# The order of tokens in the last two gate groups of each half of a streaming-encoder layer

## The chip, the cores and the metric

The kernel runs as one program on one core of a Trainium2 chip; the metric is the device time of one execution in microseconds (us). The core has a matmul engine (TensorE, PE in the rows, with its weight loads PEld), a vector engine (VectorE, DVE), an activation engine (ScalarE, ACT), a general engine (GpSimd, POOL) and SyncE (SP), whose queue issues every DMA of this kernel.

## The reference

One encoder layer over 2048 tokens of width 1024. A layer norm gives `h`. One input projection of 7592 columns feeds three branches: A, attention over the 256 keys with the highest score of a small indexer (top-k per query); B, differential attention with 4 heads; C, attention of 4 heads into 256 memory tokens. Each branch has a SiLU gate of 512 columns, an output projection to 1024 columns and a sigmoid gate of 1024 columns:

```
proj = h @ w_in[l]
...
y_a = (o_a * jax.nn.silu(a_gate)) @ w_proj_a[l]
...
g = jax.nn.sigmoid(m_gate.reshape(bsz, seq, N_BRANCH, D_MODEL))
merged = g[:, :, 0] * y_a + g[:, :, 1] * y_b + g[:, :, 2] * y_c
h = _layer_norm(DEEPNORM_ALPHA * h + merged @ w_out[l], ln_g[l], ln_b[l])
```

## The kernel before

All large matmuls are done in three parts of a high and a low half (`mm3`, lines 76 to 79: high by high, high by low, low by high), so one product is three matmuls.

The normalised input, transposed, lives in the tile `H4` (line 153; the rows call it `H`). It has room for 1024 tokens, one half of the sequence, in two parts of 512 tokens, `H4[:, 0]` and `H4[:, 1]`, each with high and low parts. The first half's tokens are computed first, stored to memory as `ht_d` (four pieces of 256 tokens and 2 MB), and the second half takes their place. At the end the second half is used up and the four pieces are read back by `reload` (line 210), two into each part of `H4`.

What the text calls gate groups are the 20 entries of `JOBS` (lines 390 to 392): 256 columns each of the C queries (`cq`, 2), the SiLU gates (`sg`, 6) and the merge gates (`tm`, 12). `gate_steps` (line 260) does one: it loads the 256 columns of weights (`load_win`, line 228: in the second half raw from memory, split into high and low by GpSimd and stored; in the first half read back in one piece of 2 MB as `w<-w_d`), and then for each part of 512 tokens of the half and each 128 columns it runs 24 matmuls of 512 columns into one of two PSUM tiles `dps`. `emit_gate` (line 313) empties it through a tile `do`, of which there are three, and SP stores that: for `tm` with one ScalarE pass, for `sg` with one more on VectorE, for `cq` with one `do` from ScalarE (line 318) and one from VectorE (line 321).

The order of the program text is: projections of half 0, top-k, projections of half 1, top-k for the blocks 8 to 15 (`topk_group`, on VectorE, ScalarE and GpSimd), then at line 793 all 20 gate groups of half 1, the four `reload`, and four gate groups of half 0. The next 12 are `fill` (line 798), steps put between the matmuls of branch B's attention by hand (`pump`, in a region in which the order of TensorE is that of the text). Branch B's tiles (`bp`, line 635) take the place of the top-k's, and its keys, values and queries (`kg`, `vg`, `bq`) are loaded there.

Then comes branch A's attention (`attn_a`, line 852, 16 blocks), what is left of `fill`, and at line 917 the last four gate groups of half 0. Between them stands the projection of the memory tokens: `gates` (line 394) calls one entry of its list `between` after each group and the rest of the list after the last group. The list is `mem_setup` (loads and transposes the memory tokens into `hm`, pool `mp`) and four times `dense_mem` (line 417: four loads of raw weights through two buffers `wr`, eight GpSimd instructions that split them into a tile `w`, 48 matmuls of 256 columns in all, two stores of `mk_d` or `mv_d`). All users of weights share two buffers `w` in turn.

Then the pools of this phase are given back and those of the next (`yp`, `yw`, `yq`, lines 921 to 923) take their place. The next phase loads the projection weights of branches B and C through tiles `yt` (eight buffers) and splits them on ScalarE and VectorE into the two parts of `H4`: `wb` into `H4[:, 0]`, `wc` into `H4[:, 1]` (lines 957 to 959). For each of 8 pairs of blocks it multiplies branch B's output by its gate (`gated`, line 937, with `yo` in one buffer), projects it (`branch`, into `yps`), then does branch C's attention and its projection.

Outside of the hand-ordered region a planner puts each engine's instructions in one fixed order: it simulates the program with its own durations and takes, at each step, the instruction that is ready with the highest priority. Priority is the order of the text, raised inside `tc.high_priority()`. So branch A's attention and the gate groups after it in the text are interleaved on TensorE, and so are branch A's attention and the phase after them. On the chip each engine runs its fixed order and waits where a datum or a buffer is late. A tile that takes the place of another waits for that tile's users alone.

Of the kernel before, what the change touches and what calls it, by code (L numbers as in the profile page):

```python
# [44 lines left out]
GB = (4, 12)  # L45
# [13 lines left out]
def tile_layer(ctx, tc, x, mem, ln_in_g, ln_in_b, w_in, w_mem_kv, diff_lambda, diff_norm_g,  # L59
# [7 lines left out]
    def split(H, L, src, eh, el):  # L67
        if eh is G:
            G.tensor_scalar(H, src, 1.0, 1.0, op0=ALU.mult, op1=ALU.mult)  # L69
        elif eh is A:  # L70
            A.copy(H, src)  # L71
        else:
            V.tensor_copy(H, src)
        el.tensor_tensor(L, src, H.bitcast(F32), op=ALU.subtract)  # L74

    def mm3(ps, lH, lL, rH, rL, start, stop):
        PE.matmul(ps, lH, rH, start=start, stop=False)  # L77
        PE.matmul(ps, lH, rL, start=False, stop=False)  # L78
        PE.matmul(ps, lL, rH, start=False, stop=stop)  # L79
# [3 lines left out]
    def dram(name, shape, dt=F32):  # L83
        return dr.tile(shape, dt, name=name)
# [59 lines left out]
    def w_view(w, r0, nk, c0, n):  # L144
        return bass.AP(tensor=w.tensor, offset=w.offset + r0 * w.shape[-1] + c0,
                       ap=[[w.shape[-1], 128], [128 * w.shape[-1], nk], [1, n]])

    def pool(name, bufs, space=None, side="left"):
        kw = {} if space is None else {"space": space}
        return tc.alloc_tile_pool(name=name, bufs=bufs, side=side, reuse_waits="tile", **kw)  # L150
# [77 lines left out]
    def load_win(cols, eh=G, el=G, rpool=None):  # L228
        w = dw.tile([128, 2, KT, 256], F32R, name="w")
        key = cols[0][0]  # L230
        if key in w_d:
            SP.dma_start(w.bitcast(F32), w_d[key])
            return w
        n = sum(c for _, c in cols)
        m = 2 if rpool is None else 4
        for i in range(0, KT, m):
            raw = (rpool or dw).tile([128, m, 256], F32, name="wr", bufs=2)
            o0 = 0
            for c0, cn in cols:
                SP.dma_start(raw[:, :, o0:o0 + cn], w_view(w_in, i * 128, m, c0, cn))  # L240
                o0 += cn
            split(w[:, 0, i:i + m, :n], w[:, 1, i:i + m, :n], raw[:, :, :n], eh, el)
        w_d[key] = dram(f"w_d{key}", [128, 2, KT, 256])
        SP.dma_start(w_d[key], w.bitcast(F32))
        return w
# [11 lines left out]
            with tc.high_priority():  # L257
                emit(kind, idx, p, ps, n)

    def gate_steps(kind, half, c0, idx):  # L260
        w = load_win([(c0, 256)])
        for q in range(2 * half, 2 * half + 2):
            for g in range(2):
                c = slice(g * 128, (g + 1) * 128)
                ps = dqs.tile([128, 512], F32, name="dps")
                for k in range(KT):
                    mm3(ps, w[:, 0, k, c], w[:, 1, k, c], H4[:, q % 2, 0, k], H4[:, q % 2, 1, k], k == 0, k == KT - 1)
                    if k == KT - 1:
                        with tc.high_priority():
                            emit_gate(kind, idx, g, q, ps)  # L270
                    yield 0.69
# [41 lines left out]
    def emit_gate(kind, idx, g, q, ps):  # L313
        if kind == "cq":
            for a in range(2):
                o = dw.tile([128, 512], F32R, name="do", bufs=3)
                if a == 0:
                    A.copy(o, ps)
                    H = o
                else:  # L320
                    V.tensor_tensor(o, ps, H.bitcast(F32), op=ALU.subtract)
                SP.dma_start(cq_d[q][:, 2 * idx + g, a], o.bitcast(F32))
            return
        r, j = idx
        o = dw.tile([128, 512], F32, name="do", bufs=3)
        A.activation(o, ps, AF.Tanh, scale=0.5)
        if kind == "sg":
            V.scalar_tensor_tensor(o, o, 1.0, ps, op0=ALU.add, op1=ALU.mult)  # L328
        SP.dma_start((sg_d if kind == "sg" else tm_d)[r][q][:, 2 * j + g], o)
# [60 lines left out]
    JOBS = [("cq", C_CQ + 256 * j, j) for j in range(2)]  # L390
# [3 lines left out]
    def gates(half, jobs, between=()):  # L394
        between = list(between)
        for i, (kind, c0, idx) in enumerate(jobs):
            yield from gate_steps(kind, half, c0, idx)
            if between:
                between.pop(0)()
        for f in between:  # L400
            f()

    def run(steps):
        for _ in steps:
            pass
# [11 lines left out]
    def dense_mem(j):  # L417
        w = dw.tile([128, 2, KT, 256], F32R, name="w")
        for i in range(2):
            for k in (4 * i, 4 * i + 2):  # L420
                raw = dw.tile([128, 2, 256], F32, name="wr", bufs=2)
                SP.dma_start(raw, w_view(w_mem_kv, k * 128, 2, 256 * j, 256))
                split(w[:, 0, k:k + 2], w[:, 1, k:k + 2], raw, G, G)
        ps = dqs.tile([128, 2, 256], F32, name="dps")
        for i in range(2):
            c = slice(i * 128, (i + 1) * 128)
            if j < 2:
                for k in range(KT):
                    mm3(ps[:, i], w[:, 0, k, c], w[:, 1, k, c], hm[0][:, 0, k], hm[0][:, 1, k], k == 0, k == KT - 1)
            else:  # L430
                for k in range(KT):
                    mm3(ps[:, i], hm[0][:, 0, k, c], hm[0][:, 1, k, c], w[:, 0, k], w[:, 1, k], k == 0, k == KT - 1)
        for i in range(2):
            o = dw.tile([128, 2, 256], F32R, name="do", bufs=3)
            if j < 2:
                split(o[:, 0], o[:, 1], ps[:, i], A, V)
                SP.dma_start(mk_d[:, 2 * j + i], o.bitcast(F32))
            else:
                h0 = 2 * (j - 2)
                ov = o.rearrange("p a (h d) -> p (a h d)", d=128).rearrange("p (h a d) -> p h a d", h=2, a=2)  # L440
                pv = ps[:, i].rearrange("p (h d) -> p h d", d=128)
                split(ov[:, :, 0], ov[:, :, 1], pv, A, V)
                SP.dma_start(mv_d[:, i, h0:h0 + 2].rearrange("p h a d -> p (h a d)"),
                             o.bitcast(F32).rearrange("p a c -> p (a c)"))
# [252 lines left out]
    class unit_b:  # L697
# [78 lines left out]
        def store(self):  # L776
# [13 lines left out]
            G.tensor_scalar(o, o, rs, None, op0=ALU.mult)  # L790
            SP.dma_start(ob_d[b][:, hd * 128:(hd + 1) * 128], o)

    run(gates(1, JOBS))
    for p in range(4):
        with tc.high_priority():
            reload(p)
    run(gates(0, JOBS[:GB[0]]))
    fill = gates(0, JOBS[GB[0]:GB[0] + GB[1]])
    owed = [0.0]

# [12 lines left out]
    with tc.manual_schedule(engines={PE.engine}):  # L813
# [5 lines left out]
        for i, u in enumerate(units):  # L819
# [8 lines left out]
            j = 0  # L828
# [85 lines left out]

    run(fill)
    mp = pool("mp", 1)
    run(gates(0, JOBS[GB[0] + GB[1]:], [mem_setup] + [(lambda j=j: dense_mem(j)) for j in range(4)]))
    mp.release()
    dqs.release()
    dw.release()  # L920
# [264 lines left out]
```

## Time and profile before

| | before |
|---|---|
| time, median of 3 runs | 2924.34 us (2923.38 to 2928.38) |
| the profiled execution | 2925.13 us, of which the span is 2923.3 us |
| TensorE busy | 2778.1 us (95%) |
| VectorE busy | 2053.1 us (70%) |
| ScalarE busy | 1401.7 us (48%) |
| GpSimd busy | 864.6 us (30%) |
| mean granted TensorE clock | 0.982 |
| moved by DMA | 476.35 MB, 163 GB/s over the span |

The time is that of the whole execution; the span is what the hardware profiler covers, from the first instruction to the last. Times in rows count from the start of the span. Busy time counts instructions of the engine itself, without waits. The granted clock is 1.00 at the upper of TensorE's two levels (2.4 GHz) and lower where part of a stretch ran at the other (1.2 GHz).

### The profile page before, as it was taken

The numbers are of one execution on the slowest core, as the hardware profiler recorded it, in microseconds if no ns is written. First come the engines' busy times: TensorE is split into PE (matmuls) and PEld (weight loads), VectorE is DVE, ScalarE is ACT, GpSimd is POOL, SyncE is SP. The second block draws the span as 40 slices with busy tenths as digits, with TensorE's granted clock in tenths as the row PEclk, the third lists the DMA queues.
The fourth block names the chain that finished last, engine by engine and source line by source line (L and its number), as shares of the span: only waits on it lengthen the run. The fifth ranks groups of instructions, "written<-read, shape, count | busy, mean of one in ns | idle before, by whom it ended". The sixth has DMA issues, their size and how long they took to land.

```text
span 2923.3 us, 49093 instructions
## 1 busy us (share of the span) xinstructions
PE 2778.1 (95%) x17488; PEld 2490.2 (85%) x17488; DVE 2053.1 (70%) x4885; ACT 1401.7 (48%) x2716; POOL 864.6 (30%) x1270
## 2 busy tenths in 40 slices
PE   6899999999999989999999998998999999988998
PEld 6799989987788877788888887887999899987887
DVE  7179978898657887677777773447777777775554
ACT  3256755774346870344444442446555655552010
POOL 7454333235433302022222323121222222211322
PEclk9999999999999999999999999999999999998999
DMA  9666555564554576434334335235333333358542
GB/s 359 233 210 237 202 179 172 169 231 171 201 173 167 190 268 203 148 114 142 109 120 131 119 99 160 97 118 170 104 104 99 118 113 111 117 170 268 198 155 73
DMA packets 332020, 476.35 MB, mean 163 GB/s; under 512 B 28928, under 2 KB 252544, under 8 KB 323584
## 3 DMA queue, kind: packets, MB, share of 16 engines
q1 hardware_dynamic: 331776, 473.23, 49.5%
q8 instruction: 138, 2.26, 0.3%
q14 instruction: 106, 0.87, 0.1%
HBM read 271.25 MB, written 201.88 MB: 162 GB/s over the span
## 4 chain that ended last, share of the span: by engine, by line
PE 68%; DMA 7%; DVE 6%; issue 3%; POOL 2%; ACT 2%; SPq 1%; POOLq 0%; DVEq 0%; ACTq 0%
PE dps L77 9%; PE dps L78 9%; PE dps L79 9%; PE ops L753 4%; PE aops L898 4%; PE apt L893 3%; PE lg L648 3%; PE lg L649 3%; PE yps L77 2%; PE yps L78 2%; PE yps L79 2%; PE pt L761 2%; PE fz L77 2%; PE fz L78 2%; PE fz L79 2%
## 5 line engine op out<-in xcount | busy, mean ns | idle before, releaser
L77 PE MATMUL dps<-H,w 128*128 128x512 f32 x1280 | 518.5, 405 | 20.0 <-DVE do L328 5.7
L78 PE MATMUL dps<-H,w 128*128 128x512 f32 x1280 | 505.6, 395 | 0.0
L79 PE MATMUL dps<-H,w 128*128 128x512 f32 x1280 | 504.2, 394 | 0.0
L77 PE MATMUL dps<-w,H 128*128 128x256 f32 (+1 forms) x1152 | 342.1, 298 | 15.4 <-ACT w L71 8.6
L79 PE MATMUL dps<-w,H 128*128 128x256 f32 (+1 forms) x1152 | 339.8, 296 | 2.3 <-DVE H L74 2.3
L78 PE MATMUL dps<-w,H 128*128 128x256 f32 (+1 forms) x1152 | 340.7, 296 | 0.8 <-POOL w L74 0.8
L556 ACT ACTIVATE ja<-sall,thr 128x1280 bf16<-128x1280 f32 (+4 forms) x224 | 301.9, 1348 | 74.7 <-DVE thr L552 69.1
L543 DVE TENSOR_SCALAR_CACHE_REDUCE jd<-sall,thr 128x1408 bf16<-128x1408 f32 (+6 forms) x231 | 330.8, 1432 | 6.3
L77 PEld LDWEIGHTS dps<-H,w 128*128 128x128 f32 x1280 | 243.8, 190 | 64.8 <-issue 9.7
L79 PEld LDWEIGHTS dps<-H,w 128*128 128x128 f32 x1280 | 243.1, 190 | 51.2
L78 PEld LDWEIGHTS dps<-H,w 128*128 128x128 f32 x1280 | 243.8, 190 | 38.2
L651 DVE CUSTOM_DVE_ANT_0 AP<-lg,bias 128x512 f32<-128x512 f32 (+3 forms) x304 | 181.8, 619 | 124.7 <-PE lg L649 61.5
L516 DVE SCALAR_TENSOR_TENSOR sall<-ir,iw,sall 128x512 f32<-128x512 f32 (+3 forms) x266 | 191.9, 768 | 70.6 <-ACT ir L512 68.1
L77 PEld LDWEIGHTS dps<-w,H 128*128 128x128 f32 x1152 | 223.5, 194 | 18.1 <-ACT w L71 9.3
L71 ACT CAST apr<-apt 128x512 fp32r<-128x512 f32 (+1 forms) x288 | 157.5, 562 | 160.7 <-PE apt L893 129.5
L79 PEld LDWEIGHTS dps<-w,H 128*128 128x128 f32 x1152 | 223.1, 194 | 3.5 <-DVE H L74 2.7
L78 PEld LDWEIGHTS dps<-w,H 128*128 128x128 f32 x1152 | 223.5, 194 | 3.0 <-POOL w L74 2.2
L74 DVE TENSOR_TENSOR apr<-apt,apr 128x512 fp32r<-128x512 f32 (+1 forms) x288 | 185.5, 656 | 57.1 <-ACT apr L71 55.4
L898 PE MATMUL aops<-apr,VA 128*128 128x256 f32 x1088 | 209.0, 299 | 14.9 <-ACT apr L71 6.5
L69 POOL TENSOR_SCALAR w<-wr 128x512 fp32r<-128x512 f32 x120 | 87.1, 734 | 424.7 <-PE dps L79 339.2
L885 ACT ACTIVATE AP<-AP,anm 128x1024 f32<-128x1024 f32 (+7 forms) x192 | 172.1, 900 | 67.7 <-DVE anm L882 64.1
L512 ACT ACTIVATE ir<-ips 128x512 f32<-128x512 f32 (+3 forms) x304 | 150.0, 550 | 105.4 <-PE ips L507 92.0
(250 smaller groups left out, 6835.9 us busy)
## 6 DMA issues: line engine op xcount, KB each, us to landing
w_d<-w SPq DMA_DIRECT2D x28, 2048.0 KB, 7.3
w<-w_d SPq DMA_DIRECT2D x28, 2048.0 KB, 8.8
wr<-in_w_in_dram SPq DMA_DIRECT2D x108, 256.0 KB, 3.3
tm_d<-do SPq DMA_DIRECT2D x96, 256.0 KB, 2.9
bq<-qb_d SPq DMA_DIRECT2D x128, 128.0 KB, 3.3
aq<-qa_d SPq DMA_DIRECT2D x128, 128.0 KB, 3.1
yt<-tm_d SPq DMA_DIRECT2D x64, 256.0 KB, 3.5
sg_d<-do SPq DMA_DIRECT2D x48, 256.0 KB, 2.6
```

What stands on the lines that cost most here:

```text
L71: A.copy(H, src)
L74: el.tensor_tensor(L, src, H.bitcast(F32), op=ALU.subtract)
L77: PE.matmul(ps, lH, rH, start=start, stop=False)
L78: PE.matmul(ps, lH, rL, start=False, stop=False)
L79: PE.matmul(ps, lL, rH, start=False, stop=stop)
L512: A.activation(r[:, :cn], ps[:, :cn], AF.Relu)
L516: V.scalar_tensor_tensor(s[:, c0:c0 + cn], r[:, :cn], iw[:, h:h + 1], s[:, c0:c0 + cn], op0=ALU.mult, op1=ALU.add)
L543: V.tensor_scalar(jd[:, :L], sc[b], t.bitcast(F32)[:, i:i + 1], None, op0=op, op1=ALU.add, accum_out=dst[:, i:i + 1])
L556: A.activation(ja[:, :L], sc[b], AF.Sign, bias=thr.bitcast(F32)[:, i:i + 1], scale=-1.0, accum_out=cnt[:, i:i + 1])
L651: V.tensor_tensor_reduce(P[:, c0:c0 + cn], ps[:, :cn], bias[:, c0:c0 + cn], scale=-0.125, scalar=-LOW, op0=ALU.add, op1=ALU.min, accum_out ...
L885: A.activation(p[:, c0:c1], p[:, c0:c1], AF.Exp, bias=nm[:, e:e + 1], scale=-1.0, accum_out=sm[:, hd, i:i + 1])
L898: PE.matmul(o_ps.rearrange("p a d -> p (a d)"), VA[:, k0 + i], pr[:, a, i].rearrange("p e q -> p (e q)"), start=(k0 + i == 0 and a == 0), ...
```

## The change

The last two gate groups of each half are taken out of `gates` and given to a new function. It loads the weights of both groups, then runs the first 512 tokens of the first group, the first 512 of the second, the second 512 of the first and the second 512 of the second. `gate_steps` takes the weights and the list of parts as arguments. Since `gates` now gets two groups at line 917 and still the list of five entries, it calls three `dense_mem` after its second group, so these stand in the text ahead of the last two gate groups.

```
-    def gate_steps(kind, half, c0, idx):
-        w = load_win([(c0, 256)])
-        for q in range(2 * half, 2 * half + 2):
+    def gate_steps(kind, half, c0, idx, w=None, qs=(0, 1)):
+        if w is None:
+            w = load_win([(c0, 256)])
+        for q in (2 * half + q for q in qs):
...
+    def gates_by_tokens(half, jobs):
+        ws = [load_win([(c0, 256)]) for _, c0, _ in jobs]
+        for q in range(2):
+            for (kind, c0, idx), w in zip(jobs, ws):
+                yield from gate_steps(kind, half, c0, idx, w, (q,))
...
-    run(gates(1, JOBS))
+    run(gates(1, JOBS[:-2]))
+    run(gates_by_tokens(1, JOBS[-2:]))
     for p in range(4):
         with tc.high_priority():
             reload(p)
...
-    run(gates(0, JOBS[GB[0] + GB[1]:], [mem_setup] + [(lambda j=j: dense_mem(j)) for j in range(4)]))
+    run(gates(0, JOBS[GB[0] + GB[1]:-2], [mem_setup] + [(lambda j=j: dense_mem(j)) for j in range(4)]))
+    run(gates_by_tokens(0, JOBS[-2:]))
     mp.release()
```

## Rows read from the trace of the kernel before

**Rows 1.** The page, part 1 and the chain's shares by engine (part 4).

```profile
PE 2778.1 (95%) x17488; PEld 2490.2 (85%) x17488; DVE 2053.1 (70%) x4885; ACT 1401.7 (48%) x2716; POOL 864.6 (30%) x1270
...
PE 68%; DMA 7%; DVE 6%; issue 3%; POOL 2%; ACT 2%; SPq 1%; POOLq 0%; DVEq 0%; ACTq 0%
```

**Rows 2.** First hand-over by stretch: length, PE, PEld, DVE, ACT, POOL, clock, DMA, GB/s.

```profile
1055.46:1066.30 10.84, 10.84 (x48) 8.64 (x47) 9.36 (x15) 8.93 (x10) 0.00 (x0) 1.00 0.92 281
1066.30:1070.90 4.60, 0.01 (x1) 0.01 (x1) 3.86 (x6) 3.87 (x4) 0.00 (x0) 0.82 1.08 362
1070.90:1084.50 13.60, 13.58 (x49) 11.01 (x50) 10.81 (x18) 9.23 (x12) 0.00 (x0) 0.81 1.11 370
1084.50:1100.28 15.78, 12.84 (x50) 10.13 (x49) 14.46 (x34) 6.83 (x8) 0.00 (x0) 0.89 0.50 198
```

**Rows 3.** The longest wait of TensorE, 990 to 1120 us: total, times, longest.

```profile
PE dps L77 <- DMA H<-ht_d: 4.6, 1, 4.6
```

**Rows 4.** SP's issues in order of time: start, us, what.

```profile
1044.59 0.32 SPq L232 DMA_DIRECT2D w<-w_d  x1
...
1055.46 3.49 SPq L211 DMA_DIRECT2D H<-ht_d  x2
...
1066.34 5.54 SPq L211 DMA_DIRECT2D H<-ht_d  x2
1071.94 6.30 SPq L232 DMA_DIRECT2D w<-w_d  x1
```

**Rows 5.** The chain that ended last, 1000 to 1300 us: start, us, what.

```profile
1056.10 14.69 DMA H<-ht_d
...
1080.45 10.43 DMA cq_d<-do
...
1177.38 5.17 DMA bq<-qb_d
1182.68 0.77 PE lg L649
```

**Rows 6.** ScalarE in order of time; in brackets idle time before, and releaser.

```profile
1079.12 0.59 ACT L318 CAST do<-dps 128x512 fp32r<-128x512 f32 x1 [2.73 <-PE dps L79]
...
1091.56 1.05 ACT L318 CAST do<-dps 128x512 fp32r<-128x512 f32 x2
```

**Rows 7.** VectorE, the end of the top-k.

```profile
1156.85 0.68 DVE L594 TENSOR_SCALAR pf<-ja 128x2048 bf16<-128x2048 bf16 x1
```

**Rows 8.** SP's issues at the start of branch B and after the gate groups.

```profile
1157.93 1.76 SPq L679 DMA_DIRECT2D kg<-kb_d  x2
...
1966.55 1.28 SPq L932 DMA_DIRECT2D yt<-in_w_proj_b_dram  x3
...
1978.20 0.67 SPq L1016 DMA_DIRECT2D yo<-ob_d  x1
```

**Rows 9.** TensorE in order of time, second hand-over.

```profile
1948.44 0.40 PE L79 MATMUL dps<-H,w 128*128 128x512 f32 x1
...
1966.23 0.28 PE L79 MATMUL dps<-w,hm 128*128 128x256 f32 x1
...
1998.04 0.60 PE L942 MATMUL cps<-idf,yo 128*128 128x128 f32 x4
...
2003.05 0.39 PE L78 MATMUL yps<-yoT,H 128*128 128x256 f32 x1 [0.88 <-POOL yoT L946]
```

**Rows 10.** Busy time by stretch, second hand-over (columns as in rows 2).

```profile
1948.67:1966.35 17.68, 17.68 (x144) 17.43 (x143) 6.75 (x17) 6.23 (x13) 7.49 (x8) 1.00 0.33 105
1966.35:2003.05 36.70, 28.07 (x162) 22.47 (x160) 30.70 (x71) 28.05 (x57) 2.55 (x2) 0.86 1.00 317
```

**Rows 11.** GpSimd, first and last split of one `dense_mem`.

```profile
1948.93 1.20 POOL L69 TENSOR_SCALAR w<-wr 128x512 fp32r<-128x512 f32 x2 [26.17 <-PE dps L79]
...
1957.82 1.29 POOL L74 TENSOR_TENSOR w<-wr,w 128x512 fp32r<-128x512 f32 x1
```

**Rows 12.** The page, part 6: a load of 256 KB, KB each, median us to landing.

```profile
yt<-tm_d SPq DMA_DIRECT2D x64, 256.0 KB, 3.5
```

## The prediction

> **What bounds the kernel now.** The page comes first: TensorE is busy for 95% of the span and holds 68% of the chain that ended last; no other engine is above 70% or 6% [rows 1]. So the time is TensorE's work plus the places where it stands still or runs at its lower clock, and the change adds or removes no matmul. Next come the two hand-overs that it touches, read by stretch.
>
> First hand-over: the last gate groups of half 1 end at 1066.30. TensorE then does nothing for 4.6 us, waiting for the read-back of `H` [rows 2, 3]. The first group of half 0 takes from 1070.90 to 1100.28, where a group takes 4 x 5.42 = 21.7 us (48 matmuls, half a group, in 10.84 us) [rows 2]. In all 1100.28 - 1066.30 - 21.7 = 12.3 us are lost: 4.6 idle, 2.9 idle in the last stretch (15.78 less 12.84), and 4.8 at the lower of the two clock levels (granted 0.81 and 0.89 after the idle times) [rows 2].
>
> Second hand-over: the last gate matmul runs at 1948.44 and the last `dense_mem` matmul at 1966.23. The loads of `wb` are issued only at 1966.55, and the first product of the next phase is complete to run at 2003.05 [rows 8, 9]. In these 36.7 us TensorE has branch A's attention alone: 28.07 us busy, granted clock 0.86 [rows 10]. Lost are 8.6 us idle and, at 14% of 28.07, 3.9 us of clock: 12.5 us.
>
> **The change, first hand-over.** *What goes.* `H4[:, 0]` becomes free two groups of 10.84 us before the end instead of one. The first two read-backs were issued at 1055.46, as soon as their part was free [rows 4], and landed 15.4 us later (0.64 us of issue and 14.69 us in the chain, 1070.8) [rows 5]. They now go at about 1044.6 and land at 1060.0, before 1066.3: the 4.6 us wait ends. The weights of the last group keep their buffer's release time. The weights of half 0's first group were issued at 1044.59, when the second last group let go of its buffer [rows 4]; that is now 1055.4, behind the read-back. At the 281 to 370 GB/s of rows 2 their 2.1 MB take 5.7 to 7.5 us from 1060.0, so they land between 1065.7 and 1067.5: 0 to 1.2 us of wait, and I take 0.
>
> *What is late next.* The other two read-backs are still issued at 1066.34, when `H4[:, 1]` is free [rows 4]. Their readers now come at 1066.3 + 10.84 = 1077.1. Landing like the first pair, 15.4 us after issue, they arrive at 1081.7: a new wait of 4.6 us at the middle of that group, and again a slow stretch after it (13.60 us for half a group after the old wait, 2.8 us more than 10.84) [rows 2]. The Trainium skill, page "DMA: Bandwidth & Descriptors", section Specifications, gives a core's share of the memory as about 358 GB/s; 4.2 MB at that rate are, as an estimate, 11.7 us, and the new wait would be 0.9 us instead of 4.6. The rows go over that figure for a moment (370 GB/s), but the pair took 15.4.
>
> The 2.9 us idle time came from the C queries' stores: they were queued behind the read-backs, took 10.43 us, and held the three `do` tiles [rows 5]. There is 4.6 us less in the queue by then, and the group is 4.6 us later in its second half; I take 1 us left, between 0 and 2.9. TensorE's loss is 4.6 + 2.8 + 1 = 8.4 us instead of 12.3, so it is 3.9 us earlier at the end of that group.
>
> *What of it reaches the end.* Very little. Branch B's first matmul waits for `bq` until 1182.68 [rows 5]. These loads begin at 1157.93, right after the top-k's last VectorE instruction ended at 1157.5 and gave up its place [rows 7, 8]. TensorE, 3.9 us earlier, only waits longer there. What counts is whether the top-k ends earlier: ScalarE stood 2.73 us in the middle of it, waiting for the late gate group [rows 6], against 0.3 us where groups come at their pace. With that group 4.6 us earlier I take 1 us from the top-k, between 3.9 (all that TensorE gains) and a loss, worked out under the third rival.
>
> **The change, second hand-over.** *What is moved.* Three `dense_mem`, with 12 raw loads, 24 GpSimd splits and 6 stores, go ahead of the last two gate groups. `hm` is then free two gate groups before the end. The issue of `wb`'s loads 0.2 us after the last use of `hm`, though `H4[:, 0]` had been free since 1948.44 at the latest, says that this is what held them [rows 8, 9]. So `wb`'s loads, and with `H4[:, 0]` free half-way its splits, fall beside gate matmuls; `wc`'s loads too, and only `wc`'s splits come after the last matmul.
>
> *What is left.* Once the last two groups have let go of `w`, the next phase needs `yo`, transposes, gate and projection, twice, since `yo` has one buffer. From the transposes at 1998.04 to the product at 2003.05 are 5.0 us [rows 9], a load of 256 KB lands in 3.5 [rows 12]: 3.5 + 0.6 + 3.5 + 5.0 = 12.6 us at the least. At the most it is the 24.9 us from the first `yo` issue to the product as before [rows 8, 9]. I take 16, nearer to the lower end: before, the DMA ran at 317 GB/s through 36.7 us, 11.6 MB, of which the 4.2 MB of `wb` and `wc` now pass earlier [rows 10]. Alone, branch A's attention lost 12.5/36.7 = 34% of TensorE's time, clock included, or 23% without. So 16 x 0.34 = 5.4 us are lost instead of 12.5: 7.1 us gained, between 4.0 (24.9 x 0.34) and 9.6 (12.6 x 0.23).
>
> *What could be uncovered.* Three `dense_mem` in a row have no gate group under which their weights are split. A split takes 10.2 us from first to last [rows 11]; two `dense_mem` with branch A's share took TensorE 17.68 us, 8.8 each [rows 10]. Short by 1.4 us each, at most 4 us in all, and branch A's matmuls fill most of it: I take 0.
>
> **Sum.** 7.1 + 1 = 8.1 us off the profiled execution's 2925.13, or 2917.0; that execution is 0.8 us above the median of 2924.34, so the forecast is 2916. That the gain stays: after 2003 branch A's attention and the next phase share TensorE, whose work is unchanged.
>
> **The rivals.**
> *Half of it* (22%). The next phase starts no sooner than its own loads of 7.4 MB (11.6 less 4.2) allow, 24.9 us after the last gate; the gain is 4.0, and nothing passes the top-k: 2920. For it: the DMA share was 1.00 in that stretch [rows 10]. Against it: only `yo` and the gate are needed for the first product.
>
> *Both places pay* (15%). TensorE's 3.9 us arrive because the top-k ends that much earlier, and the attention alone, freed of 8 splits on two engines, loses nothing at the second place: 3.9 + 12.5 = 16.4, 2908. For it: VectorE and ScalarE were busy 30.7 and 28.1 of 36.7 us there [rows 10].
>
> *Slower: the top-k is held up* (13%). ScalarE runs in its fixed order. Before, the first group's second copy stood behind the last pass of the top-k and ran at 1091.56, when a store of the C queries had landed (1080.45 + 10.43) [rows 5, 6]. With the group ready at 1077.1 the planner may put that copy ahead of a pass. Then ScalarE stands until about 1090.9, the top-k and branch B's loads are up to 13.8 us later, and against 7.1 gained the kernel needs 2931. It is slower than before from a hold of 7.1 us on. The Trainium skill, page "TensorE: Matmul & The Clock Gate", table of its head, calls the queue of ScalarE strictly first in, first out; the 2.73 us wait for a matmul in the midst of the top-k agrees [rows 6]. Against it: the planner left that copy behind the passes once.
>
> **How the numbers follow.** The forecast (50%, its own range 2911 to 2920) and the rivals above. A measurement of this kernel tells 0.2%, 5.8 us, from no change, so the bounds are 2918.5 and 2930.2. Faster: 38 of the forecast's 50, the 15, and 4 of the half's 22, 57%. Slower: the third rival beyond its threshold, 8, and 5 out of the other cases for a new plan of everything behind the change that fits the chip worse, 13%. The rest, 30%, is within. Range: 2906, past the best case, to 2928, in the middle of the third rival's cases.
>
> **What would show it.** The step at 1066 is right if TensorE goes on there without a wait and waits some 4 us for `H` a half group later; it is wrong if it waits for `w`. `kg`'s first issue says what the top-k did: 1157 if I am right, near 1170 for the third rival. At the second place `wb`'s loads have to be issued before the last gate matmul, and the first projection some 16 us after it instead of 36.7 after `dense_mem`. Wrong would be a copy of ScalarE for `dps` that waits for a `cq_d` store, waits for `w` in the three `dense_mem`, or an order on TensorE that leaves branch A's attention without other work elsewhere.

## The result and the profile after

The kernel after takes 2902.38 us (median of 4 runs, 2899.63 to 2905.72) against 2925.2 us (4 runs, 2923.38 to 2928.38) before: a ratio of 0.9936, 95% interval 0.9917 to 0.9956. That is 0.64% or 18.7 us by the ratio, 22.8 us by the medians. The forecast was 2916 with a range of 2906 to 2928: the sign was right, the gain was more than twice the 8.1 us of the sum, and the median lies 3.6 us below the range. The profiled execution of after took 2899.8 us with a span of 2898.0, 25.3 us less than the span before.

Part 1 of the page after and its chain shares answer to [rows 1]. TensorE's busy time fell by 10.5 us although it runs the same 17,488 matmuls. Its mean granted clock rose from 0.982 to 0.985, which over the two spans is some 9 us, so most of that part of the gain is clock.

```profile
PE 2767.6 (95%) x17488; PEld 2486.4 (86%) x17488; DVE 2053.2 (71%) x4885; ACT 1401.0 (48%) x2716; POOL 861.0 (30%) x1270
...
PE 68%; DMA 7%; DVE 7%; issue 3%; POOL 2%; ACT 2%; SPq 0%; DVEq 0%; POOLq 0%; ACTq 0%
```

**First hand-over.** SP's issues in order of time, to be laid beside [rows 4, 8]: one pair of read-backs now goes 11.5 us earlier (1043.96), the second pair at nearly the old time (1065.72 for 1066.34), and half 0's first weights 10.3 us later (1054.85). The top-k's end moves by 0.4 us only: `kg` at 1157.51 for 1157.93.

```profile
1043.96 3.67 SPq L211 DMA_DIRECT2D H<-ht_d  x2
...
1054.85 0.32 SPq L232 DMA_DIRECT2D w<-w_d  x1
...
1065.72 2.83 SPq L211 DMA_DIRECT2D H<-ht_d  x2
...
1157.51 2.46 SPq L686 DMA_DIRECT2D kg<-kb_d  x2
```

TensorE in the same stretch (start, us, what; in brackets the idle time before it and what ended it). The 4.6 us of [rows 3] are gone; in their place stand three waits of 1.0, 3.0 and 2.5 us. The second is labelled with a VectorE instruction of the top-k. But the matmul is the first to read the second part of `H`, whose last load is on the trace as landed at 1080.80, 15.1 us after the pair's issue, and its PSUM tile had been emptied 7 us before: it waited for the read-back. After it the matmuls run at 0.63 us each for a time, instead of 0.39 to 0.40.

```profile
1066.72 0.47 PE L77 MATMUL dps<-H,w 128*128 128x512 f32 x1 [1.03 <-DMA w<-w_d]
...
1077.50 0.39 PE L79 MATMUL dps<-H,w 128*128 128x512 f32 x1
1080.89 0.47 PE L77 MATMUL dps<-H,w 128*128 128x512 f32 x1 [3.01 <-DVE thr L559]
...
1083.26 0.63 PE L79 MATMUL dps<-H,w 128*128 128x512 f32 x1
...
1090.72 0.50 PE L77 MATMUL dps<-H,w 128*128 128x512 f32 x1 [2.50 <-DVE do L322]
```

**Second hand-over.** SP's issues, beside [rows 8]: `wb` is loaded from 1895.07 on and `wc` from 1928.62, all of it before the last gate matmul at 1965.32; the first `yo` goes at 1970.78.

```profile
1895.07 0.53 SPq L941 DMA_DIRECT2D yt<-in_w_proj_b_dram  x1
...
1905.34 0.33 SPq L941 DMA_DIRECT2D yt<-in_w_proj_b_dram  x1
...
1928.62 2.10 SPq L941 DMA_DIRECT2D yt<-in_w_proj_c_dram  x4
...
1970.78 0.43 SPq L1025 DMA_DIRECT2D yo<-ob_d  x1
...
1980.46 4.42 SPq L1025 DMA_DIRECT2D yo<-ob_d  x2
```

TensorE there, beside [rows 9]: transposes of the second `yo` at 1983.86, projections running from 1988.01, where it was 2003.05.

```profile
1965.32 0.39 PE L79 MATMUL dps<-H,w 128*128 128x512 f32 x1
...
1983.86 0.66 PE L951 MATMUL cps<-idf,yo 128*128 128x128 f32 x4 [0.72 <-DMA yo<-ob_d]
...
1988.01 0.28 PE L78 MATMUL yps<-yoT,H 128*128 128x256 f32 x1
```

**What no row ahead of the prediction covers: everything after.** I cut the time from branch B's last logits to the end at three matmuls: the first `yps` (projections of B and C begin), the last `yps` (they end), the first `fz` (the output projection begins). Columns: stretch and length, busy PE, PEld, DVE, ACT, POOL, clock, DMA share, GB/s. The kernel before:

```profile
1777.00:2001.80 224.80, 208.42 (x1207) 179.86 (x1206) 101.70 (x257) 92.35 (x178) 37.78 (x53) 0.96 0.48 156
2001.80:2593.30 591.50, 574.11 (x4447) 542.85 (x4445) 439.31 (x1222) 346.12 (x813) 141.32 (x142) 1.00 0.36 107
2593.30:2668.50 75.20, 59.05 (x409) 55.17 (x409) 40.71 (x108) 24.45 (x64) 9.18 (x7) 0.86 0.82 262
2668.50:2923.30 254.80, 244.37 (x1338) 209.13 (x1336) 141.38 (x213) 28.93 (x48) 65.69 (x57) 0.99 0.47 153
```

The kernel after:

```profile
1774.10:1987.20 213.10, 201.46 (x1179) 175.28 (x1178) 97.37 (x249) 89.69 (x172) 38.85 (x53) 0.98 0.49 162
1987.20:2568.30 581.10, 571.22 (x4438) 540.62 (x4436) 437.78 (x1204) 343.63 (x804) 140.50 (x142) 1.00 0.37 109
2568.30:2646.90 78.60, 61.75 (x448) 58.44 (x447) 44.29 (x136) 28.67 (x79) 9.44 (x7) 0.89 0.78 240
2646.90:2898.00 251.10, 241.84 (x1335) 208.02 (x1333) 143.03 (x214) 29.64 (x49) 63.88 (x57) 0.99 0.48 159
```

Of the 25.3 us, 2.9 are there at the end of branch B (1777.0 against 1774.1). The first stretch is 11.7 us shorter: 4.7 of TensorE's idle time, and 7.0 of busy time. Of the latter, 3.7 are only put off: there are 28 matmuls fewer, all of branch A's attention (24 transposes and products that follow each other at 0.11 to 0.12 us, and 4 logits at 0.23). The other 3.3 I put down to the clock (0.96 and 0.98). So the hand-over itself gave 8.0 us. The other three stretches are 10.7 us shorter with 3.7 us more work in them, 14.4 us net: 7.5 of idle time in the second, 0.5 in the last two, and 6.4 of busy time for the same work. The last I put down to the clock as well, though to two digits the rows show it changed in the third alone (0.86 and 0.89). **More than half of the gain lies behind the place that was changed.**

TensorE's waits in the second stretch (total, times, longest) of the kernel before:

```profile
PE cps L942 <- DMA yo<-ob_d: 3.9, 6, 1.3
PE aops L898 <- ACT apr L71: 3.7, 6, 1.4
PE lg L648 <- DVE amx L651: 3.4, 7, 0.7
```

And of the kernel after, where the wait for ScalarE's `apr` is not among the seven largest:

```profile
PE cps L951 <- DMA yo<-ob_d: 2.5, 5, 0.7
PE aops L906 <- DVE apr L74: 1.9, 7, 0.4
...
PE lg L655 <- DVE amx L658: 0.9, 4, 0.3
```

Branch A's attention has smaller waits for its own softmax there. The tiles and the work are the same; the orders that the planner gave the engines are not. Cut by the eight pairs of blocks, the idle time that is gone lies in the first pair (4.7 us before, 1.4 after) and in the third to the sixth (9.9 before, 3.8 after). The third to the sixth, before and after:

```profile
2165.18:2469.32 304.14, 294.21 (x2265) 278.17 (x2264) 222.03 (x605) 177.16 (x412) 71.06 (x72) 0.99 0.37 108
2151.89:2433.75 281.86, 278.10 (x2170) 264.36 (x2169) 211.82 (x561) 165.56 (x388) 69.92 (x71) 1.00 0.37 111
```

### The profile page after: what moved, and what is told of

It reads as the page before. It is cut to its first block, busy times and chain, and to the rows that moved or that the text cites. A ratio compares the mean times of both kernels' runs of the same rounds, so it can differ in the third digit from the quotient of the medians.

```text
span 2898.0 us, 49105 instructions
## 1 busy us (share of the span) xinstructions
PE 2767.6 (95%) x17488; PEld 2486.4 (86%) x17488; DVE 2053.2 (71%) x4885; ACT 1401.0 (48%) x2716; POOL 861.0 (30%) x1270
## 4 chain that ended last, share of the span: by engine, by line
PE 68%; DMA 7%; DVE 7%; issue 3%; POOL 2%; ACT 2%; SPq 0%; DVEq 0%; POOLq 0%; ACTq 0%
PE dps L77 9%; PE dps L78 9%; PE dps L79 9%; PE ops L760 4%; PE aops L906 4%; PE apt L901 3%; PE lg L655 3%; PE lg L656 3%; PE pt L768 2%; PE yps L77 2%; PE yps L78 2%; PE yps L79 2%; PE fz L77 2%; PE fz L79 2%; PE fz L78 2%
## 5 line engine op out<-in xcount | busy, mean ns | idle before, releaser
L906 PE MATMUL aops<-apr,VA 128*128 128x256 f32 x1088 | 202.9, 294 | 11.8 <-DVE ao L916 6.2
L893 ACT ACTIVATE AP<-AP,anm 128x1024 f32<-128x1024 f32 (+7 forms) x192 | 172.2, 899 | 75.9 <-DVE anm L890 75.2
L734 ACT ACTIVATE P<-P,nm 128x2048 f32<-128x2048 f32 (+15 forms) x128 | 154.4, 1206 | 85.8 <-DVE nm L733 85.7
```

What stands on the lines that cost most here:

```text
L734: A.activation(p[:, :L], p[:, :L], AF.Exp, bias=nm[:, c:c + 1], scale=-1.0, accum_out=sm[:, c:c + 1])
L893: A.activation(p[:, c0:c1], p[:, c0:c1], AF.Exp, bias=nm[:, e:e + 1], scale=-1.0, accum_out=sm[:, hd, i:i + 1])
L906: PE.matmul(o_ps.rearrange("p a d -> p (a d)"), VA[:, k0 + i], pr[:, a, i].rearrange("p e q -> p (e q)"), start=(k0 + i == 0 and a == 0), ...
```

## The experiments

Twelve kernels, each timed beside the kernel before (medians of 2922.6 to 2923.5 us there; the table's first two lines are from the comparison above). The column "left" counts in TensorE's fixed order how many of the 2944 matmuls and transposes of branch A's attention stand behind the last `yps`. The other columns come from each profile: start of the first `yps`; TensorE's idle time between first and last `yps`, and from there to the end; granted clock between the last `yps` and the first `fz`; time from the last `yps` to the first `fz`, and from A's last `aops` matmul to it.

| kernel | left | first yps | idle, shared | idle, after | clock | C to fz | A to fz | median, us | ratio |
|---|---|---|---|---|---|---|---|---|---|
| before | 94 | 2001.8 | 17.4 | 26.6 | 0.86 | 75.2 | 39.1 | 2925.2 | 1 |
| after | 130 | 1987.2 | 9.9 | 26.1 | 0.89 | 78.6 | 25.2 | 2902.4 | 0.9936 |
| e1: half 1 alone | 94 | 2001.4 | 17.5 | 26.7 | 0.91 | 73.0 | 37.8 | 2922.3 | 0.9994 |
| e2: half 0 alone | 130 | 1995.3 | 10.4 | 25.7 | 0.87 | 80.3 | 27.1 | 2908.5 | 0.9944 |
| e3: memory ahead alone | 24 | 1993.8 | 15.1 | 27.2 | 0.76 | 57.2 | 45.8 | 2924.0 | 0.9998 |
| e4: token order alone | 24 | 2002.6 | 19.3 | 26.8 | 0.79 | 56.0 | 44.9 | 2928.2 | 1.0011 |
| e5: before, pair 7 first | 168 | 2001.3 | 17.1 | 23.9 | 0.91 | 79.8 | 20.7 | 2916.0 | 0.9977 |
| e6: e3, pairs 6 and 7 first | 196 | 1992.0 | 16.1 | 31.0 | 0.87 | 96.4 | 22.6 | 2924.1 | 0.9999 |
| e7: after, pairs 3 to 7 later | 51 | 1988.3 | 11.7 | 26.5 | 0.88 | 68.8 | 49.7 | 2907.8 | 0.9946 |
| e8: after, pair 7 first | 196 | 1991.6 | 13.3 | 31.4 | 0.89 | 94.4 | 20.7 | 2912.5 | 0.9960 |
| e9: e3, A first | 130 | 1986.3 | 9.6 | 25.7 | 0.89 | 78.8 | 25.7 | 2903.4 | 0.9933 |
| e10: after, A first | 130 | 1981.7 | 9.9 | 26.4 | 0.91 | 77.7 | 28.1 | 2898.5 | 0.9922 |
| e11: before, late A first | 24 | 1996.6 | 17.3 | 29.3 | 0.76 | 57.3 | 45.9 | 2928.7 | 1.0028 |
| e12: after, pair 7 raised a little | 154 | 1987.7 | 9.4 | 21.6 | 0.91 | 75.2 | 20.1 | 2897.9 | 0.9920 |

### The parts of the change by themselves (e1 to e4)

Half 1 alone: the diff's lines for half 1, half 0 as before.

> Only the last two gate groups of half 1 by tokens; half 0 as before. The changed kernel's trace shows branch B's attention 3 us earlier at its end and no earlier at its first matmul. If that is the first hand-over's whole share (my theory): 2922 us, 3 less than before, first projection of the next phase 3 us earlier (2000), phase that branch A shares with B and C 590 us long as before. Rival, that the 10 us gained in that shared phase are a new plan's luck and have nothing to do with the second hand-over: the shared phase has another length here too, by 5 us or more either way.

2922.34 us, ratio 0.9994 (0.9984 to 1.0004): the time that my theory gave, and the shared phase has its old length (590.0 us). Apart from the half groups that the edit swaps, TensorE's order is that of the kernel before from start to end. The read-backs come earlier and nearly nothing of it arrives: branch B's attention ends at 1776.1, 0.9 us earlier and not 3.

Half 0 alone: the diff's lines for half 0, half 1 as before.

> Only the second hand-over changed (the last two groups of half 0 by tokens, three memory projections ahead of them). My theory, that the two places add: 2925 - 22 = 2903 us, 12 of it before the first projection and 10 in the shared phase after it. Rival, that the shared phase was luck of the plan: 2913.

2908.54 us, ratio 0.9944 (0.9929 to 0.9959), which overlaps the whole change's interval. The time lies midway between the 2903 and the 2913 that were expected and does not decide between them. The trace does: apart from the swapped half groups of half 1, TensorE's order is the same as after the change, and so are the 10 us of idle time in the shared phase. Nearly all of the gain is half 0's.

The memory projection ahead alone: the two groups in their old order, half 1 as before.

```
-    run(gates_by_tokens(0, JOBS[-2:]))
+    run(gates(0, JOBS[-2:]))
```

> The three memory projections ahead of the last two groups of half 0, but these two groups one after the other as before: no order by tokens anywhere. Theory M, that the early release of hm, which held the loads of wb, is what pays at the second hand-over: within 4 us of e2_half0, about 2905, loads of wb issued near 1895 to 1900, first projection near 1990. Theory T, that the order by tokens pays, because it frees the first part of H early: 2920 to 2925, first projection near 2000.

2923.96 us, ratio 0.9998 (0.9988 to 1.0009): no gain, as theory T had it, though `wb` was loaded from 1900.49 on and the first `yps` came 8.0 us earlier than before, nearer to theory M. That the memory projection ahead is enough for the whole gain falls; what it gave was lost again behind it.

The token order alone: three `dense_mem` put back behind the last groups, half 1 as before.

```
-    run(gates(0, JOBS[GB[0] + GB[1]:-2], [mem_setup] + [(lambda j=j: dense_mem(j)) for j in range(4)]))
+    run(gates(0, JOBS[GB[0] + GB[1]:-2], [mem_setup, lambda: dense_mem(0)]))
     run(gates_by_tokens(0, JOBS[-2:]))
+    for j in range(1, 4):
+        dense_mem(j)
```

> The last two groups of half 0 by tokens, with the three memory projections behind them instead of ahead. Theory M: the loads of wb wait for hm until the end of the last memory projection as before, and there are now three projections in a row at the end with nothing beside them but branch A's attention: 2922 to 2932, first projection 2000 or later. Theory T: about 2905, as e2_half0.

2928.19 us, ratio 1.0011 (0.9999 to 1.0024), within theory M's range: that the token order is what gains falls too. Neither part of half 0's change gains anything alone; together they gain 15 us. That the parts don't add up pointed at the orders: both parts tried alone leave 24 of A's matmuls behind C's last projection, the kernel after 130.

### How much of branch A is left when C ends (e5 to e8)

From here on the text of the hand-overs stays as it is in the kernel named, and only priorities change. First theory R: the more of A is left to cover the loads of the last phase, the better. e5 puts the last pair of the shared phase first in the planner:

```
     for p in range(NP):
         T = []
+        ctx = tc.high_priority() if p >= 7 else contextlib.nullcontext()
+        with ctx:
...
```

> The kernel before, with one edit: the last of the eight pairs of blocks of the shared phase (branches B and C) has the highest priority in the planner. Nothing at either hand-over changes. In TensorE's planned order 168 matmuls and transposes of branch A's attention stand behind the last projection of C, against 94 before, 130 after the change and 24 in the two halves tried alone that gained nothing (the memory projection ahead without the token order, and the token order without the memory projection ahead). Theory R (reserve): what of A's attention is left when C's projections end covers the loads of the last phase, so its amount decides some 15 us of the time: from the first projection to the end 920 us before (94), 910 after (130), 924 to 927 in the two halves (24), 0.14 us for each. R expects 910 us or less from there: 2914, between 2909 and 2918. Theory H (the change's gain is the hand-over alone, the halves lost to chance in their plans): 2924, between 2919 and 2929.

2915.99 us, ratio 0.9977 (0.9967 to 0.9986): 7 us gained with both hand-overs untouched. Theory H falls; the plan behind the hand-over is worth time by itself. The time is within R's range, though from the first `yps` to the end it takes 912.9 us and not 910 or less.

e6 is e3 with `p >= 6`.

> The memory projection ahead of the last two gate groups of half 0, without the token order (2924 when tried alone), and the last two pairs of the shared phase at the highest priority: 196 of A's matmuls are left behind C's last projection, where the one tried alone left 24. The hand-over is not touched: first projection at about 1995, where it is 2003 before. R expects 908 us from there on: 2905, between 2900 and 2911, so the memory projection ahead is worth its 8 us at the hand-over without any token order. H', that the token order itself is needed (wb's and wc's loads between the gates): 2922, between 2917 and 2927.

2924.11 us, ratio 0.9999 (0.9988 to 1.0011). R falls, and H' is within its range. With 196 left, C ends 21 us earlier than in e3, but A's last `aops` matmul comes only at 2651.5 and the first `fz` at 2674.1.

e7 is the kernel after with a lower priority for late pairs (`tc.high_priority(offset=-20000) if p >= 3`).

> The kernel after the change, both hand-overs as they are, with the pairs 3 to 7 of the shared phase at a lower priority: 51 of A's matmuls are left behind C's last projection instead of 130. R expects about 80 x 0.14 = 11 us of the gain to go: 2913, between 2909 and 2919. H expects it to stay at 2902, between 2898 and 2906.

2907.77 us, ratio 0.9946 (0.9933 to 0.9960): 5 us above after by the medians, half of what R expected, with intervals that overlap. It decides nothing.

e8 is the kernel after with e5's edit.

> The kernel after the change with the last pair of the shared phase at the highest priority: 196 of A's matmuls are left behind C's last projection instead of 130. If R holds beyond 130: 2902 less up to 66 x 0.14 = 9 us, 2893 to 2900. If the loads of the last phase are covered with 130 already (TensorE's granted clock was 1.00 in the 46 us after C's last projection and fell to 0.69 for 20 us only then): 2899 to 2904. H expects 2902.

2912.53 us, ratio 0.9960 (0.9945 to 0.9974): against the kernel after 10 us lost by the medians, 7 by the ratios, where no theory expected a loss. From the last `yps` to the first `fz` it takes 94.4 us with 24.0 of them idle, against 78.6 and 16.9 after. That row, and the one that follows it:

```profile
2569.60:2664.00 94.40, 70.45 (x519) 66.68 (x518) 58.99 (x176) 39.29 (x105) 11.62 (x9) 0.89 0.73 219
2664.00:2913.00 249.00, 241.56 (x1327) 209.20 (x1327) 137.40 (x207) 25.70 (x42) 59.74 (x55) 0.99 0.47 157
```

So too much left costs time too: e6 and e8 have the most idle time behind C's end, 31.0 and 31.4 us. The intervals of e8 and of the kernel after overlap at their edges; that of e12 below lies clear of e8's. That made theory U: the first `fz` comes no sooner than about 57 us after C's end (for its loads, as I took it) and about 21 us after A's end, and the best amount makes neither late. The columns "C to fz" and "A to fz" have no value below 56.0 and 20.1 in all fourteen kernels; where 24 are left the first stands near its least value, from 154 on the second. What sets these two values was not tried.

### Theory U, tested (e9 to e12)

e9 is e3, without any token order, and with branch A's attention raised:

```
-    for b in range(NB - 1, -1, -1):
-        attn_a(b)
+    with tc.high_priority():
+        for b in range(NB - 1, -1, -1):
+            attn_a(b)
```

> The memory projection ahead of the last two gate groups of half 0, without the token order, and all of branch A's attention at the highest priority in the planner. Tried without the latter this gave 2924; with it the plan leaves 130 of A's matmuls behind C's last projection, as after the change, where it left 24. Theory U (the plan behind the hand-over, with a best amount of A left over: the last phase's first product comes no sooner than about 21 us after A's end and 57 us after C's end, and between 130 and 168 neither is late; and the token order acts only by the plan that comes of it): first projection near 1994, 910 to 914 us from there, 2906, between 2900 and 2912. Theory K (the token order of half 0 is itself what gains): 2923, between 2918 and 2928.

2903.36 us, ratio 0.9933 (0.9920 to 0.9946). U expected 2906, K 2923. The memory projection ahead needs no token order; it needs a plan that keeps what it gave. The first `yps` came at 1986.3 instead of near 1994, so raising A's attention changed the stretch ahead of it as well. The stretches behind the first `yps`:

```profile
1986.30:2569.70 583.40, 573.79 (x4466) 544.35 (x4464) 441.78 (x1215) 349.38 (x811) 140.78 (x142) 1.00 0.36 108
2569.70:2648.50 78.80, 61.01 (x450) 57.69 (x448) 45.42 (x138) 29.90 (x81) 9.04 (x7) 0.89 0.78 242
2648.50:2897.30 248.80, 240.94 (x1335) 208.17 (x1332) 142.38 (x212) 28.38 (x47) 63.84 (x57) 0.99 0.48 160
```

Those of e3, the same text without the raised priority: 5.5 us more idle in the first of them, and only 40.72 us of work for TensorE beside the loads, at a granted clock of 0.76:

```profile
1993.80:2598.30 604.50, 589.38 (x4558) 555.70 (x4557) 457.45 (x1300) 361.46 (x859) 141.52 (x142) 1.00 0.36 107
2598.30:2655.50 57.20, 40.72 (x247) 36.25 (x245) 26.68 (x43) 12.30 (x24) 9.52 (x7) 0.76 0.85 284
2655.50:2921.80 266.30, 255.61 (x1429) 222.45 (x1429) 146.26 (x219) 31.62 (x52) 62.33 (x57) 0.98 0.47 155
```

e10 is the kernel after with the same edit.

> The kernel after the change with the same priority for branch A's attention: 130 left over, as without it. The control of the run before: U and K both expect 2902, between 2897 and 2908. If this one and the run before agree within 4 us, the token order of half 0 is worth nothing beside the memory projection ahead; if this one is 10 us or more faster, K.

2898.50 us, ratio 0.9922 (0.9908 to 0.9937). It is 4.9 us below e9 by the medians and 3.2 by the ratios, with intervals that overlap. That is neither within the 4 us nor near the 10 that were to decide, though much nearer to U. The two differ in both token orders, which by the scatter of six executions each are worth anything from nothing to some 9 us beside the memory projection ahead.

e11 is the kernel before with A's last ten blocks raised (`range(9, -1, -1)` under `tc.high_priority()`).

> The kernel before, hand-overs untouched, with branch A's last ten blocks at the highest priority: 24 of A's matmuls are left behind C's last projection instead of 94, as in the two halves that gained nothing. U: 4 to 8 us slower than before, 2929, between 2925 and 2935. K, and that the plan there counts for nothing: 2923, between 2919 and 2927.

2928.73 us, ratio 1.0028 (1.0018 to 1.0038): slower, as U expected, with the hand-overs of before. The profiled execution (2925.24 us) is the fastest of the eleven, so its stretches do not show the whole loss. The stretch from the last `yps` to the first `fz` looks like that of e3:

```profile
2598.30:2655.60 57.30, 40.53 (x246) 36.28 (x244) 27.21 (x42) 12.09 (x24) 8.36 (x7) 0.76 0.86 282
```

e12 is the kernel after with e5's edit at `tc.high_priority(300)`.

> The kernel after the change with the last pair of the shared phase raised a little (by 300 places of the text) instead of to the top: 154 left over, between the 130 of the kernel after and the 196 that cost 10 us. U: A ends some 60 us after C, no later than with 168 in the kernel before, which gained 7 us: 2900, between 2896 and 2904. If any raise of that pair costs: 2907 to 2912.

2897.94 us, ratio 0.9920 (0.9906 to 0.9935), the fastest median of all, though its interval does not set it apart from the kernel after. Idle time from the last `yps` to the first `fz` is 75.20 - 64.34 = 10.9 us, against 16.9 after:

```profile
2565.00:2640.20 75.20, 64.34 (x472) 60.32 (x471) 48.45 (x152) 30.45 (x85) 8.94 (x7) 0.91 0.83 250
```

## Why the prediction was right, and where it fell short

**First hand-over: right, and worth as little as it said.** The 4.6 us wait went, the second pair became late at the middle of the group, and most of the loss came back in other waits: 1.0 us for `w` (I took 0 of a bound of 1.2), 3.0 for `H` (I took 4.6), 2.5 in the middle of the second half group (I took 1). From the last gate matmul of half 1 to the end of that group TensorE lost some 9 us, where I took 8.4, against 12.3 before. The Trainium skill, page "DMA: Bandwidth & Descriptors", section Specifications, with its 358 GB/s, made the second of these waits 0.9 as an estimate. The pair took 15.1 us from issue to landing, near the 15.3 that [rows 5] add up to for the pair before. The top-k ended 0.4 us earlier instead of 1, and branch B's first load set its start as before. e1 puts the whole at a gain of 0.06%, between a gain of 0.16% and a loss of 0.04%. The 2.9 us lead at branch B's end is no contradiction: in e2, e3, e4 and e11, whose TensorE order is that of the kernel before up to there, that point lies anywhere from 1772.2 to 1780.5, so 2.9 us tell nothing.

**Top-k held up: no.** The planner did put copies of the C queries ahead of passes of the top-k, as the third rival feared. But the copy in front waited 1.09 us for its matmul, less than the 2.73 of [rows 6], and the one at 1087.71, which stood behind the last pass before, found everything ready. ScalarE in order of time:

```profile
1072.48 0.59 ACT L319 CAST do<-dps 128x512 fp32r<-128x512 f32 x1 [1.09 <-PE dps L79]
...
1087.71 0.56 ACT L319 CAST do<-dps 128x512 fp32r<-128x512 f32 x1
1088.17 2.00 ACT L563 ACTIVATE ja<-sall,thr 128x2048 bf16<-128x2048 f32 x1
```

**Second hand-over: right in mechanism; the size came out by two errors that offset each other.** `wb` is loaded from 1895.07 on, 0.8 us after the last use of `hm` began (1894.3), so `hm` was what held it; in e4, where the memory projection comes last, it is loaded from 1969.41 on only. `wb` and `wc` are loaded and, but for the last piece, split beside the gates. Three `dense_mem` in a row leave TensorE no gap (32.30 of 32.30 us busy from 1862.0 to 1894.3). The gain is 8.0 us where I took 7.1. But the time from the last gate matmul to the projections is 22.7 us, not 16, and in it TensorE stands still for 3.7 us at a granted clock of 1.00, 16% of it and not 34%: 3.7 us lost where I took 5.4. The length was missed at the load of `yo`, which I took at the 3.5 us of [rows 12]: the first landed at 1979.72, 8.9 us after its issue, next after the loads of `yt`, `mkT` and `mv` that were issued ahead of it. Since `yo` has one buffer, the second was issued only at 1980.46, behind the transposes of the first. Why that stretch loses less per microsecond than before was not tried. Its row:

```profile
1965.32:1988.01 22.69, 19.03 (x125) 15.70 (x123) 18.23 (x46) 14.03 (x29) 2.57 (x2) 1.00 0.78 250
```

**The step that failed** is the last sentence of the sum, "that the gain stays: after 2003 branch A's attention and the next phase share TensorE, whose work is unchanged". The work is unchanged; its order is not, and with the order went 14.4 us: idle time in the shared phase (17.4 to 9.9 us), and busy time that I put down to the clock. I had seen a new plan only as 5 chances in 100 of a loss. Priorities alone, with the hand-overs left as they are, move the kernel before by -7 us (e5) and +6 us (e11), and set two versions of the kernel after 14.6 us apart by the medians, 11.7 by the ratios (e8, e12). e3, beside e9, shows that a new plan can eat the hand-over's gain whole. So the sign and the hand-over were foreseen; that the median lies 3.6 us below the range was not.

**What stays open.** The amount of A that is left can explain only the smaller part of those 14.4 us. It acts behind C's end, and there the kernel after gains some 4 us: 36 matmuls more at some 0.12 us, in 0.3 us less time. In the table it does not go with the idle time of the shared phase: with half 0 as before that is 17.1 to 17.5 us at 24, 94 and 168 left (e11; before and e1; e5), with half 0 as after 9.4 to 13.3 at 51, 130, 154 and 196 (e7; after, e2 and e10; e12; e8). Why the shared phase idles for 9 to 13 us in some plans and 15 to 19 in others was not isolated. It is a property of the plan and no accident of one execution: before and e1, with one TensorE order, have 17.4 and 17.5; after and e2, with another, 9.9 and 10.4. It sits where raising a late pair does not reach: TensorE's order in e5 leaves that of the kernel before, and in e8 that of the kernel after, only in the seventh pair, and the third to the sixth idle for 9.6 and 4.8 us, about as in the kernel that each comes from:

```profile
2164.62:2466.79 302.17, 292.58 (x2265) 276.54 (x2264) 221.85 (x605) 177.05 (x412) 71.13 (x72) 1.00 0.37 109
2156.42:2439.09 282.67, 277.86 (x2171) 264.29 (x2169) 211.76 (x561) 165.57 (x388) 70.03 (x71) 1.00 0.37 110
```

But no run moved it by itself: in e9 the left-over changed with it. So it is not known whether that part of the gain was luck of the plan or follows from half 0's new text. How much of the 6.4 us of busy time behind the hand-over belongs to which cause was not tried either.

## What to carry to other kernels

Where a planner orders the engines, an edit of the text has two effects: the local one, which can be read from the stretch around it, and a new order of everything behind it, which here was larger than the local one and, in other plans of the same work, had either sign. Give the second its own width in the forecast, compare the two programs' fixed orders before believing a local story, and try parts of a change together with a neutral change of priorities before calling a part useless. When two phases overlap, look at how much of the older one is left when the newer ends: here 196 left gave the most idle time behind that point (31 us), 154 and 168 the least (21.6 and 23.9), and 24 left the lowest clock while the next phase loaded (0.76 to 0.79).

## What the runs showed of the hardware

In the kernel after, a 3.0 us wait of TensorE was followed, after six matmuls at 0.39 to 0.48 us, by eight of 128x512 at 0.54 to 0.63 us; the granted clock from 1077.90 to 1088.30 was 0.84. So here the lower clock came a little after the idle time, and its price fell on work that waits for nothing. In e3, 20 us right behind C's last projection, in which TensorE had 14.42 us of work, ran at a granted clock of 0.57; over its whole transition from the last `yps` to the first `fz` the clock was 0.76 with 40.72 us of work in 57.20, in e12 0.91 with 64.34 in 75.20. A load of `yo` in the kernel after, issued behind some 10 us of other loads, took 8.9 us to land, and the next one 3.4. The row of e3:

```profile
2600.00:2620.00 20.00, 14.42 (x63) 11.74 (x64) 9.22 (x16) 5.33 (x13) 3.99 (x3) 0.57 0.75 235
```
